# Gather, transform, scatter-add: later sort passes and smaller first one-hot groups

## The chip, the cores and the metric

The kernel runs on one core of one Trainium2 chip. The metric is the device time of one execution in microseconds (us). Times below are those of five runs (their median counts) and of one further, profiled execution, in which every instruction has a start and a duration.

## What is computed

A graph with 4096 nodes of 256 features and 262,144 edges: each edge carries its source node's features through a matrix, and the results are summed at its destination.

```python
def reference(nodes, edges_src, edges_dst, w_msg, w_self):
    N, D = nodes.shape
    self_out = nodes @ w_self
    src_feat = nodes[edges_src]
    msg = src_feat @ w_msg
    agg = np.zeros((N, D), dtype=np.float32)
    np.add.at(agg, edges_dst, msg)
    return (self_out + agg).astype(np.float32)
```

Node and weight values are normal random numbers, the edges' ends uniform random integers.

## The kernel before

**Idea.** The messages are first made per node, not per edge: Y = nodes · w_msg, in bf16. What is left is a sum over edges of rows of Y, which is a product of a matrix of edge counts with Y. The count matrix is cut into 352 *runs* (NRUN): 11 segments of 374 destinations (SW) by 32 blocks (NB) of 128 sources. Edges are sorted by run and destination. They lie in 2048 *chunks* of 128 edges, so that a chunk touches a narrow window of one or two runs. For each chunk the vector engine (DVE) makes two one-hot matrices, e (edge by source within its block, 128 wide) and d (edge by destination offset, 110 wide), and the tensor engine (PE) multiplies them into a window of the run's counts in PSUM.

**Stage 1, sort (to about 160 us of the span).** Edge keys stand as a 128 x 2048 fp32 array, and min/max passes on the DVE (`mm`, L746 and L749) with rotations by the PE bring them close to order. The last passes, SORT_S, work on two halves: chunks 0 to 1023 (XS) and 1024 to 2047 (XL). `_Sort.run` issues those of the first half at once. Those of the second half are 16 passes of one min and one max, 32 instructions; they are not issued but kept in the list `sort.late`.

**Stage 2, chunks.** One Python loop over c = 0 to 2047 writes out the order of all engines by hand (`manual_schedule`: each engine's instructions run in the order of the program). In it:

- `onehots(c, n)` makes the one-hots of a *group* of n chunks. `sizes` lists the groups: 8, 8, 16, three of 32, then 64s. A group of 32 or more takes per one-hot one subtraction (L396, `e_off` or `d_off`) and 8 (e) or 7 (d) comparisons (L402). e and d have three buffers each, one group to a buffer whatever its size, so the DVE can be at most three groups ahead. At some chunks (`split_at`), `split_vals` (L372, L373) first splits sorted keys `vals` into the two columns that the comparisons read.
- Sort passes of the second half: from group c = LATE_FROM on, four instructions of `sort.late` (LATE_STEP) stand behind each group's one-hots. At group LATE_SUB the list is empty, and `late.bases` (k16, the lowest key of each chunk, and gi) and `late.subtract` (L300) follow.
- `turn_late(0)`, at the clear of run SHIFT, and `turn_late(1)`, at chunk LATE_TURN, transpose the second half's keys by four PE instructions each into a free bank of the PSUM ring; ACT reads them into `vals` (L312). `late.total` is one more ACT pass over them (L343), for a test at the end. From run SHIFT on the ring of six banks is turned by one bank, so that one bank is free for the transposes.
- `late.places`, ten small DVE instructions, computes from gi the PSUM addresses (`poff`) of chunks 1024 and on. It stands ahead of group LATE_USE.
- For each chunk a matmul adds e^T d into the ring (L425). Runs are cleared ahead (a matmul by zeros, also L425), and evicted by ACT to bf16 buffers atr (L481) when the last chunk that can touch them is done; POOL issues a DMA that adds the overlap of a run into the next one (L501); 46 chunks later (LAG) the PE multiplies the run by Y into the output (L524, L519), to which nodes · w_self is added at the start of a segment (L513). Finished segments go out in 12 stores each on the SP queue, paced by later evictions.

**Behind the loop** stands a test whether the approximate sort was good enough, and a general path if not. Its instructions are placed among those of the loop by the framework's scheduler: k16 is written to DRAM (kd, L625) and read back shifted by one chunk (kn, L629) by DMAs on the SP queue, and the DVE's gn and v (L633, L635) read kn. In the kernel before, L633 and L635 stand directly behind the first e_off after the second half's `subtract`, and the second half's kd follows 27 output stores on the SP queue. In the changed kernel they stand behind the first e_off after `subtract` as well, and kd follows 36 output stores.

Of the kernel before, what the change touches and what calls it, by code (L numbers as in the profile page):

```python
# [24 lines left out]
NB = 32  # L25
JB = 16
HALF = 1024
SHIFT = 148
LATE_FROM = 256
LATE_STEP = 4  # L30
LATE_SUB = 768
LATE_TURN = 872
LATE_USE = 960
NSEG = 11
NRUN = NSEG * NB
OFF = 6 * (NB - 1)
# [47 lines left out]
def kernel(  # L84
# [14 lines left out]
    NCOL = E // P  # L99
# [81 lines left out]
    for (c0, c1), (d64, s64) in zip(PIECES, ld):  # L181
        dlo = d64[:].bitcast(I32)[:, 0::2]
        slo = s64[:].bitcast(I32)[:, 0::2]
        c = slice(c0, c1)
# [69 lines left out]
    sort = _Sort(nc, tc, psum_sort, XA, (XS, XL), id2, zw)  # L254
# [16 lines left out]
    class Half:  # L271
# [47 lines left out]
        def places(self):  # L319
# [6 lines left out]
            if self.h == 0:  # L326
                stt(
                    out=sl[:, c], in0=rhoc[:, c], scalar=float(SHIFT - OFF), in1=sl[:, c],
                    op0=ALU.is_ge, op1=ALU.add,
# [44 lines left out]

    split_at = {0: 64, 64: 512, 512: HALF, HALF: HALF + 256, HALF + 256: NCOL}

    sizes = [8, 8, 16, 32, 32, 32] + [64] * ((NCOL - 128) // 64)
    assert sum(sizes) == NCOL

    def onehots(c, n):  # L380
        res = []
        if c in split_at:
            split_vals(c, split_at[c])
        for nm, val, wid, row in (("e", slo_b, P, jrow), ("d", rel_b, W, drow)):
            o = ohp.tile([P, 32, wid, 2], BF16, name=nm + "_oh", tag=nm, bufs=3)
            v = val[:, c:c + n].rearrange("p (g i) -> p g i", i=2).unsqueeze(2)
            if n < 32:
                shp = [P, n // 2, wid, 2]
                tt(
                    out=o[:, 0:n // 2], in0=v.to_broadcast(shp),  # L390
                    in1=row[:].unsqueeze(1).to_broadcast(shp), op=ALU.is_equal,
                )
            else:
                u = ohp.tile([P, 32, JB, 2], I16, name=nm + "_off", tag="off", bufs=2)
                shp = [P, n // 2, JB, 2]
                tt(  # L396
                    out=u[:, 0:n // 2], in0=v.to_broadcast(shp),
                    in1=row[:, 0:JB, :].unsqueeze(1).to_broadcast(shp), op=ALU.subtract,
                )
                for j in range(0, wid, JB):  # L400
                    w = min(JB, wid - j)
                    tss(  # L402
                        out=o[:, 0:n // 2, j:j + w, :], in_=u[:, 0:n // 2, 0:w, :],
                        scalar=float(-j), op=ALU.is_equal,
                    )
            res.append(o)
        return res
# [5 lines left out]
    def clear_at(r):  # L413
        return min(max(line(at, r) for at in CLEAR[0:3]), line(CLEAR[3], r))

    def evac_at(r):
        return min(line(at, r + 1) for at in EVAC)
# [6 lines left out]
    def count_mm(ap, lhsT, rhs, start, after=()):  # L424
        mm = nc.tensor.matmul(  # L425
            out=ap, lhsT=lhsT, rhs=rhs, start=start, stop=True, skip_group_check=True,
        ).ins
        tc.declare_no_dep(
            mm, group="evac", keep=after, reason="disjoint banks by static schedule"
        )  # L430
        for i in after:
            tc.add_manual_dep(mm, i.name, DEP, reason="bank free")
        tc.add_to_no_dep_group("count", mm)
        last_mm[0] = mm
        return mm

    def bank(r):
        return (r + (r >= SHIFT)) % RING * BW

    def bank_free(slot):  # L440

        old = slot - RING
        if old == SHIFT:
            return [late_read[-1]]
        return [evac_of[old - (old > SHIFT)]] if old >= 0 else []

    late_read = []

    def turn_late(t):
        b = bank(SHIFT - 1) // BW  # L450
        b = (b + 1) % RING * BW
        mms, act = late.turn(t, ring[:, b:b + BW])
        for m in mms:
            after = bank_free(SHIFT) if t == 0 else [late_read[-1]]
            tc.declare_no_dep(
                m.ins, group="evac", keep=after, reason="disjoint banks by static schedule"
            )
            for i in after:
                tc.add_manual_dep(m.ins, i.name, DEP, reason="bank free")
            tc.add_to_no_dep_group("count", m.ins)  # L460
        ins = act.ins
        tc.declare_no_dep(
            ins, group="count", keep=[m.ins for m in mms], reason="disjoint banks by static schedule"
        )
        tc.add_manual_dep(ins, mms[-1].ins.name, DEP, reason="transposed")
        tc.add_to_no_dep_group("evac", ins)
        late_read.append(ins)

    def clear(r):
        b = bank(r)  # L470
        after = bank_free(r + (r >= SHIFT))
        zone = bass.AP(
            tensor=ring.tensor, offset=ring[:, b:b + 1].offset,
            ap=[list(ring[:].ap[0]), [SW + W - GAP, 2], [1, GAP]],
        )
        count_mm(zone, zer[:, 0, :], zer[:, 1:3, 0:GAP], True, after)

    def evac(r):
        at = ats[r % NAT]
        b = bank(r)  # L480
        ins = nc.scalar.copy(out=at[:, 0:SW + W], in_=ring[:, b:b + SW + W]).ins  # L481
        tc.declare_no_dep(
            ins, group="count", keep=[last_mm[0]], reason="disjoint banks by static schedule"
        )
        tc.add_manual_dep(ins, last_mm[0].name, DEP, reason="run complete")
        tc.add_to_no_dep_group("evac", ins)
        evac_of[r] = ins
        at_of[r] = at
# [4 lines left out]
    def by_dma(r):  # L493
        return r < NRUN - 8 and r // 2 % 6 > 0
# [54 lines left out]
    if True:  # L549
        todo = []  # L550
        regs = []
        ncl = 0
        nev = 0
        rest = sort.late
        starts = {}
        c = 0
        for n in sizes:
            starts[c] = n
            c += n
        for c in range(NCOL):  # L560
            if c in starts:
                c0 = c
                if c == LATE_USE:
                    late.places()
                e, d = onehots(c, starts[c])
                if c >= LATE_FROM:
                    for _ in range(LATE_STEP):
                        if rest:
                            rest.pop(0)()
                if c == LATE_SUB:  # L570
                    assert not rest
                    late.bases()
                    for t in range(2):
                        late.subtract(t)
            if c == LATE_TURN:
                turn_late(1)
                late.total()
            ci = c - c0
            while ncl < NRUN and clear_at(ncl) <= c:
                if ncl == SHIFT:  # L580
                    turn_late(0)
                clear(ncl)
                ncl += 1
            if c % 8 == 0:
                regs = [nc.tensor.alloc_register(f"po{c}_{i}") for i in range(8)]
                q, h8 = c % HALF // G8, c // HALF * G8
                nc.tensor.load(regs, poff[q:q + 1, h8:h8 + 8])
            addr = nc.tensor.snap(
                regs[c % 8], donate=True, min_val=PSUM0, max_val=PSUM0 + 4 * (RING * BW - W)
            ).with_bounds(  # L590
                min_val=PSUM0, max_val=PSUM0 + 4 * (RING * BW - W),
                guaranteed_mod_val=0, out_of_modulus=4,
            )
            off = (addr - PSUM0) // 4
            count_mm(
                ring[:, bass.ds(off, W)], e[:, ci // 2, :, ci % 2], d[:, ci // 2, :, ci % 2], False
            )
            for _ in range(FILL.get(c + 1, 0)):
                nc.tensor.matmul(  # L599
                    out=out_ps[:, 2:4, :], lhsT=zw[:, 0:P], rhs=zw[:], start=True, stop=True,  # L600
                    skip_group_check=True,
                )
            while nev < NRUN and (evac_at(nev) <= c or c == NCOL - 1):
                evac(nev)
                if nev % 2 == 0 and nev and by_dma(nev - 1):
                    merge(nev - 2)
                todo.append((c + LAG + (SWITCH if nev % NB == 0 else 0), nev))
                if nev % 2 and stores:
                    dst, src = stores.pop(0)
                    tc.add_manual_dep(  # L610
                        nc.sync.dma_start(dst, src).ins, evac_of[nev].name, DEP, reason="pace"
                    )
                nev += 1
            while todo and (todo[0][0] <= c or c == NCOL - 1):
                apply_run(todo.pop(0)[1])
# [382 lines left out]
```

## Time and profile before

| | |
|---|---|
| five runs | median 484.42 us, 481.81 to 488.24 |
| profiled execution | 483.58 us, span 481.8 us |
| mean TensorE clock in it | 0.959 |
| DVE busy | 416.2 us, 884 instructions |
| PE busy | 379.6 us, 4098 instructions |
| ACT busy | 240.5 us, 459 instructions |
| POOL busy | 195.2 us, 190 instructions |

The span runs from the first instruction to the last. A view called slices cuts it in 40 equal parts and gives each engine's busy share in tenths. The waits say for whom an engine stood idle and how long. The timeline lists instructions by start time, in us of the span: start, duration, engine, line, operation, what is written and read with the shapes, count, and in brackets the idle time before it and what ended it. Busy shares are averages over stages with different limits, so each stage must be read for itself.

### The profile page before, as it was taken

The page shows a single profiled execution, that of the slowest core. Times are in us where ns is not written, and L with a number is a line of the kernel's source. Part 1 is how long each engine was busy: PE and PEld are TensorE (multiplying, and loading weights), DVE is VectorE, ACT ScalarE, POOL GpSimd, SP SyncE. Part 2 cuts the span into 40 slices and gives each one's busy share as a digit, 9 for nine tenths or more (in the row PEclk, how much of TensorE's full clock was granted, in tenths as well). Part 3 has the DMA queues.
Part 4 walks back from the last instruction along what each step waited for, and adds up shares of the span by engine and source line. Part 5 has one row for each costly group of instructions (what it writes and reads, how often), then busy time and mean ns, then how long its engine had stood idle before and what let it go on. Part 6 is the DMA issues. An engine that isn't in the chain of part 4 may idle for free.

```text
span 481.8 us, 10985 instructions
## 1 busy us (share of the span) xinstructions
PE 379.6 (79%) x4098; PEld 310.4 (64%) x4107; DVE 416.2 (86%) x884; ACT 240.5 (50%) x459; POOL 195.2 (41%) x190
## 2 busy tenths in 40 slices
PE   0009736989871798987987987899999999999994
PEld 0004232745540468986876976789988899998893
DVE  8999999899899999999999997999978688897400
ACT  3100010322281236765654765577777677777771
POOL 4200000000000035764564675276667675776760
PEclk9999896999996799999998999899999999999999
DMA  8893111111000023443333334244544453545451
GB/s 324 119 180 110 27 26 25 28 23 27 12 0 0 0 16 26 31 48 38 31 41 35 36 30 58 26 45 44 53 42 52 40 57 36 56 40 56 38 60 40
DMA packets 66306, 23.78 MB, mean 49 GB/s; under 512 B 52170, under 2 KB 64970, under 8 KB 66250
## 3 DMA queue, kind: packets, MB, share of 16 engines
q0 software_dynamic: 43872, 10.42, 26.7%
q1 hardware_dynamic: 21548, 10.42, 8.2%
q10 hardware_dynamic: 830, 2.20, 1.2%
q8 instruction: 34, 0.56, 0.5%
q14 instruction: 22, 0.18, 0.1%
HBM read 8.92 MB, written 6.30 MB: 32 GB/s over the span
## 4 chain that ended last, share of the span: by engine, by line
DVE 44%; PE 40%; DMA 6%; issue 4%; POOL 2%; ACT 2%; SPq 0%; DVEq 0%; ACTq 0%; POOLq 0%
PE ring L425 15%; PE out_ps L524 13%; DVE XA L749 13%; DVE e_oh L402 8%; DVE d_oh L402 7%; PE warm L786 6%; DVE XS L749 6%; DVE XL L746 4%; DMA atr<-atr 3%; POOL atr L501 2%; PE tp_sw L892 2%; DMA d<-in_edges_dst_dram 2%; DVE d_off L396 2%; DVE e_off L396 1%; PE out_ps L599 1%
## 5 line engine op out<-in xcount | busy, mean ns | idle before, releaser
L501 POOL DMA_DIRECT2D atr<-atr x163 | 186.4, 1259 | 264.2 <-ACT atr L481 261.1
L481 ACT CAST atr<-ring 128x484 bf16<-128x484 f32 x352 | 192.3, 565 | 105.0 <-PE ring L425 84.1
L425 PE MATMUL ring<-d_oh,e_oh 128*128 128x110 bf16 x2048 | 196.3, 215 | 19.9 <-DVE d_oh L402 16.7
L425 PEld LDWEIGHTS <-e_oh 128*128 128x128 bf16 x2048 | 164.4, 98 | 25.6 <-issue 15.5
L524 PE MATMUL out_ps<-Y,atr 128*128 128x256 bf16 x1056 | 172.5, 275 | 2.2 <-DMA atr<-atr 2.2
L402 DVE TENSOR_SCALAR e_oh<-e_off 128x1024 bf16<-128x1024 int16 (+1 forms) x264 | 98.9, 445 | 20.5 <-PE ring L425 18.5
L786 PE MATMUL warm<-zw 128*128 128x512 bf16 x169 | 55.1, 421 | 65.6 <-DVE XA L749 49.9
L749 DVE TENSOR_TENSOR XA<-XA 128x510 f32<-128x510 f32 (+35 forms) x142 | 97.1, 731 | 5.0 <-ACT XA L896 3.3
L524 PEld LDWEIGHTS <-atr 128*128 128x128 bf16 x1056 | 90.7, 98 | 9.5 <-DMA atr<-atr 3.0
L425 PE MATMUL ring<-zer 128*128 128x204 bf16 x352 | 88.5, 252 | 1.4 <-ACT atr L481 1.3
L402 DVE TENSOR_SCALAR d_oh<-d_off 128x1024 bf16<-128x1024 int16 (+3 forms) x231 | 87.0, 446 | 1.1
L786 PEld LDWEIGHTS <-zw 128*128 128x128 bf16 x176 | 17.3, 102 | 99.6 <-issue 54.8
L896 ACT COPY XA<-tp_sw 128x512 f32<-128x512 f32 x24 | 14.2, 593 | 92.1 <-PE tp_sw L892 91.4
L425 PEld LDWEIGHTS <-zer 128*128 128x128 bf16 x352 | 34.4, 98 | 9.5 <-issue 6.9
L749 DVE TENSOR_TENSOR XS<-XS 128x512 f32<-128x512 f32 (+17 forms) x40 | 29.0, 770 | 2.6 <-ACT XS L950 2.0
L746 DVE TENSOR_TENSOR XL<-XL 128x1196 f32<-128x1196 f32 (+15 forms) x32 | 28.1, 918 | 0.3
L892 PEld LDWEIGHTS tp_sw<-XA,id 128*128 128x128 f32 x192 | 22.4, 190 | 5.2 <-issue 2.4
L892 PE MATMUL tp_sw<-XA,id 128*128 128x128 f32 x192 | 23.9, 277 | 2.1 <-DVE XA L749 2.1
L396 DVE TENSOR_TENSOR e_off<-slo_b,jrow 128x1024 int16<-128x1024 int16 (+1 forms) x33 | 21.6, 655 | 0.0
L396 DVE TENSOR_TENSOR d_off<-rel_b,drow 128x1024 int16<-128x1024 int16 (+1 forms) x33 | 21.5, 652 | 0.0
L643 DVE COPY bsum<-ring 1x3 f32<-1x3 f32 x1 | 0.1, 149 | 24.1 <-PE ring L642 24.1
L519 PE MATMUL out_ps<-Y,atr 128*128 128x256 bf16 x65 | 17.8, 274 | 0.0
(104 smaller groups left out, 153.4 us busy)
## 6 DMA issues: line engine op xcount, KB each, us to landing
atr<-atr POOLq DMA_DIRECT2D x123, 55.0 KB, 2.8
out_dram<-o_sb SPq DMA_DIRECT2D x110, 32.0 KB, 1.6
nodes_bf<-in_nodes_dram POOLq DMA_DIRECT2D x1, 2048.0 KB, 15.8
nodes_bf_dram<-nodes_bf SPq DMA_DIRECT2D x1, 2048.0 KB
atr<-atr POOLq DMA_DIRECT2D x40, 27.5 KB, 2.9
s<-in_edges_src_dram ACTq DMA_DIRECT2D x2, 512.0 KB
d<-in_edges_dst_dram SPq DMA_DIRECT2D x2, 512.0 KB, 8.1
XT<-nodes_bf_dram SPq DMA_TRANSPOSE x64, 2.4
```

The lines of the kernel that those rows point to most:

```text
L396: tt(out=u[:, 0:n // 2], in0=v.to_broadcast(shp), in1=row[:, 0:JB, :].unsqueeze(1).to_broadcast(shp), op=ALU.subtract,)
L402: tss(out=o[:, 0:n // 2, j:j + w, :], in_=u[:, 0:n // 2, 0:w, :], scalar=float(-j), op=ALU.is_equal,)
L425: mm = nc.tensor.matmul(out=ap, lhsT=lhsT, rhs=rhs, start=start, stop=True, skip_group_check=True,).ins
L481: ins = nc.scalar.copy(out=at[:, 0:SW + W], in_=ring[:, b:b + SW + W]).ins
L501: nc.gpsimd.dma_start(out=atr[:, b:b + n, 0:W], in_=atr[:, a:a + n, SW:SW + W], accum_op=ALU.add)
L519: nc.tensor.matmul(out=out_ps[:, 0, :], lhsT=spill[:, SW:SW + P], rhs=Y[:, b, :], start=False, stop=False, skip_group_check=True,)
L524: nc.tensor.matmul(out=out_ps[:, t, :], lhsT=at[:, t * P:(t + 1) * P], rhs=Y[:, b, :], start=False, stop=(b == NB - 1), skip_group_check=True,
L746: self.defer.append(lambda: self.nc.vector.tensor_tensor(out=out, in0=in0, in1=in1, op=op))
L749: self.nc.vector.tensor_tensor(out=out, in0=in0, in1=in1, op=op),
L786: self.nc.tensor.matmul(out=w[:], lhsT=self.zw[:, 0:P], rhs=self.zw[:], start=True, stop=True).ins
L892: self.nc.tensor.matmul(out=tp[:, g * P:(g + 1) * P], lhsT=self.turned(rots[8 * h + 4 * t + g]), rhs=sel(x)[:, 4 * t + g], start=True, sto ...
L896: self.nc.scalar.copy(out=sel(y)[:, 4 * t:4 * t + 4], in_=tp[:].rearrange("p (g i b) -> p g i b", g=4, b=bb),)
```

## The change

The sort passes of the second half stand behind later groups. They are no longer four to a group from 256 on: after group c of n chunks, (c + n - 352) / 544 of the 32 instructions are due. With the new group sizes these are 5, 4, 4, 3, 4, 4, 4 and 4, behind groups 384, 448, 512, 576, 640, 704, 768 and 832; before, they were four each behind the groups 256 to 704. bases and subtract stand behind group 896 instead of 768. The run at whose clear the ring is turned and the first four transposes stand is 165 instead of 148, which puts them at chunk 957 instead of 857; the other four are at 970 instead of 872. places stands ahead of group 1024 instead of 960. Chunks 128 to 319 and 1024 to 1151 are made in groups of 32 instead of 64, which are ten groups for five. Nothing else changes.

```diff
-SHIFT = 148
-LATE_FROM = 256
-LATE_STEP = 4
-LATE_SUB = 768
-LATE_TURN = 872
-LATE_USE = 960
+SHIFT = 165
+LATE_FROM = 352
+LATE_SUB = 896
+LATE_TURN = 970
...
-    sizes = [8, 8, 16, 32, 32, 32] + [64] * ((NCOL - 128) // 64)
+    sizes = [8, 8, 16] + [32] * 9 + [64] * 11 + [32] * 4 + [64] * 14
...
-        rest = sort.late
+        ops, done = sort.late, 0
...
-                if c == LATE_USE:
+                if c == HALF:
                     late.places()
                 e, d = onehots(c, starts[c])
                 if c >= LATE_FROM:
-                    for _ in range(LATE_STEP):
-                        if rest:
-                            rest.pop(0)()
+                    due = len(ops) * (c + starts[c] - LATE_FROM) // (LATE_SUB - LATE_FROM)
+                    for op in ops[done:due]:
+                        op()
+                    done = max(done, min(due, len(ops)))
                 if c == LATE_SUB:
-                    assert not rest
+                    assert done == len(ops)
                     late.bases()
```

## The prediction

> **What bounds the kernel now.** I read the span in slices first. The vector engine (DVE) is full from the start to about slice 26, and only then is the tensor engine (PE) full.
>
> ```profile
> PE   0009736989871798987987987899999999999994
> DVE  8999999899899999999999997999978688897400
> ```
> (A slice is 12.05 us. Slices 13 to 26, 160 to 320 us, are the ones that the change touches.) The waits of 160 to 482 us tell who starves whom; columns are total us, times, longest:
>
> ```profile
> DVE e_oh L402 <- PE ring L425: 18.5, 13, 3.2
> PE ring L425 <- DVE d_oh L402: 16.7, 10, 3.1
> DVE gn L633 <- DMA kn<-kd: 2.7, 1, 2.7
> ```
> Ten times the PE waits for one-hots, 13 times the DVE waits for the PE to free a buffer. The timelines separate them: all PE waits lie between 166 and 302 us, all DVE ones after 339 us. This is the last wait of the PE:
>
> ```profile
> 301.56 0.26 PE L425 MATMUL ring<-d_oh,e_oh 128*128 128x110 bf16 x2 [2.77 <-DVE d_oh L402]
> ```
> Counting ring matmuls, it is the start of chunk 832. So up to chunk 832 the DVE's queue sets the pace, from there the PE does (180 us to the end). At chunk 960 the DVE's one-hots were ready 5.7 us before the PE came, at 1024 7.2 us. The question is only whether the DVE's sum of work ahead of *any* group shrinks, and which group is the last that the PE waits for.
>
> The DVE's timeline prices its pieces (start, duration, then the group):
>
> ```profile
> 178.19 0.41 DVE L396 TENSOR_TENSOR e_off<-slo_b,jrow 128x512 int16<-128x512 int16 x1
> 178.71 1.71 DVE L402 TENSOR_SCALAR e_oh<-e_off 128x512 bf16<-128x512 int16 x8
> 182.19 0.68 DVE L396 TENSOR_TENSOR e_off<-slo_b,jrow 128x1024 int16<-128x1024 int16 x1
> 189.37 0.68 DVE L396 TENSOR_TENSOR e_off<-slo_b,jrow 128x1024 int16<-128x1024 int16 x1
> 203.51 5.22 DVE L746 TENSOR_TENSOR XL<-XL 128x1196 f32<-128x1196 f32 x4
> 208.64 0.69 DVE L396 TENSOR_TENSOR e_off<-slo_b,jrow 128x1024 int16<-128x1024 int16 x1
> 290.57 1.29 DVE L300 SCALAR_TENSOR_TENSOR XL<-XL,gi 128x512 f32<-128x512 f32 x2
> 295.18 0.18 DVE L633 TENSOR_SCALAR gn<-kn 128x16 int32<-128x16 int32 x1 [2.71 <-DMA kn<-kd]
> ```
> A group of 32 chunks takes 4.00 us from its e_off to the next (178.19 to 182.19); a group of 64 takes 7.18 (182.19 to 189.37), 7.1 as the mean of 14 such groups. The eight quartets of sort passes take 5.13, 4.53, 3.64, 3.27, 3.04, 2.84, 2.67, 2.57 us: 27.7 in all.
>
> [...] from start to start, a 1024-element L402 takes 338 ns in the median, a 512-element one 202, so half the elements cost 60%. [...] of the three 32-chunk groups two took 4.00 us, and the one under which POOL issued three DMAs 5.07. [...] Here the clock fell after waits of 3.15, 2.81 and 2.77 us, not after 2.33: windows of 10 us at 220 and 230 us show 0.85 and 0.98, which is 3.4 us at half speed, 1.7 us lost.
>
> **The change part by part.** (1) *Six new 32-chunk groups for three 64-chunk ones* (chunks 128 to 320), and *four for two* at 1024 to 1152. POOL's disturbance is per chunk: 64-chunk groups average 0.6 over their undisturbed 6.5, so I take 4.0 + 0.3 = 4.3 per 32 (bounds 4.0 and 5.07, the two measured). The early part then costs the DVE 6 x 4.3 - 3 x 7.1 = +4.5 us (+2.7 to +9.1), on the path. What is gained is that the PE may start on half a group: its 1.62 us wait at chunk 128 goes.
>
> (2) *Sort passes.* The formula puts 5, 4, 4, 3, 4, 4, 4, 4 of them behind groups 384 to 832; before it was four each behind 256 to 704. They are moved by two groups, hardly spread. No DVE work is saved; what is ready ahead of them is ready earlier, what follows is not.
>
> (3) *bases and subtract* (289.34 to 291.78, 2.45 us) go from group 768 to 896. With them goes the wait at L633: the gn of the closing test still stands behind the next e_off and waits for kd and kn, two DMAs in series that begin when k16 is done (290.36; landed 295.1). It stays 2.7 us (0 to 5). In SP's queue they now follow 36 stores instead of 27; the 36th is paced by run 127's eviction, near chunk 756, long past. The stores behind them have no reader on chip.
>
> (4) *places* (ten small instructions, 1.56 us with those of the test between them) goes behind group 960, where the DVE will wait for vals anyway: -1.56 ahead of 960.
>
> (5) *Transposes.* Two times four on the PE (0.45 us each) at chunks 957 and 970 instead of 857 and 872, and three ACT instructions (0.69, 0.69, 1.15 + 0.19) with them. 17 evictions of 0.565 us move ahead of them on ACT. Before, the eviction after total came late and the PE waited 1.30 us for its bank at 311.94; I move this cost, too. New is a DVE wait: split_vals of chunk 1024 now needs the ACT read that follows PE chunk 970. Queued behind it are all later one-hots; who waits is the PE at 1024.
>
> The recurrence, in us of the span: DVE ready = previous ready + passes behind it + 7.1 (+0.45 for a split_vals); PE start = the later of that and previous start + 8.5 (the PE's 64 chunks, waits taken out, over 320 to 1024), +1.7 after a wait over 2.7. Chunk 128's group starts on the DVE at 182.2, so 320's at 182.2 + 25.8 = 208.0.
>
> | chunk | passes before it | DVE ready | PE arrives | PE starts | before |
> |---|---|---|---|---|---|
> | 320 | 0 | 215.1 | 213.4 | 215.1 | 215.9 |
> | 384 | 0 | 222.2 | 223.6 | 223.6 | 227.3 |
> | 448 | 6.3 | 235.6 | 232.1 | 235.6 | 238.3 |
> | 512 | 4.3 | 247.5 | 245.8 | 247.5 | 248.8 |
> | 576 | 3.55 | 258.1 | 256.0 | 258.1 | 259.9 |
> | 640 | 2.45 | 267.7 | 266.6 | 267.7 | 270.5 |
> | 704 | 3.05 | 277.8 | 276.2 | 277.8 | 279.8 |
> | 768 | 2.85 | 287.8 | 286.3 | 287.8 | 289.5 |
> | 832 | 2.7 | 297.6 | 296.3 | 297.6 | 301.6 |
> | 896 | 2.55 | 307.2 | 306.1 | 307.2 | 314.0 |
> | 960 | 2.45 + 2.7 + 0.3 | 319.8 | 316.2 | 319.8 | 323.0 |
>
> The 6.8 us ahead at 896 are half lost at 960: with the passes, bases and the kn wait so late, the PE waits 3.6 us there, and its clock falls. 1024: the PE arrives at 319.8 + 8.5 + 0.45 + 1.3 + 1.7 = 331.7 (before 331.9). Its chunk 970 is reached some 2.1 us after 319.8; transposes 0.9 at half clock, ACT 1.0, split_vals 0.45, 4.3: one-hots ready at 328.5, so the new wait (bound: 0 to 2 us of PE time, as ACT may be two evictions late) costs nothing; PE work of 960 covers it. Then 332.8, 337.1, 341.4 and, for the 64-chunk group 1152, 348.5; the PE needs 8.0 + 8.4 us for 128 chunks and arrives at 348.1. It starts at 348.5, before 348.3. From there both kernels do the same with the DVE ahead.
>
> **Sum:** +0.2 us on a span of 481.8; the profiled run took 483.58 (1.8 outside the span) and the median of five is 484.42, 0.8 above it. Forecast: 484.42 + 0.2 = **484.6**.
>
> **Rivals.**
> - *Much slower: the 32-chunk groups cost as the disturbed one, 5.07.* One mechanism, at ten groups: POOL's DMAs hold up twice as many instructions. For: the only group measured beneath three POOL issues. Against: two of three at 4.00, and issues come per run, not per instruction. Each 0.1 us costs up to 1.0; from 4.8 us per group it decides (+5 us, 489.6); at 5.07, 492.3. Chance 0.14.
> - *Faster: the DVE's lead holds to 960.* If kn lands before gn asks for it and 32-chunk groups run at 4.0, 960 is ready at 319.8 - 2.7 - 1.8 = 315.3, where the PE arrives at 314.4 and keeps its clock; with 8.5 + 0.45 + 1.3 and 16.45 it reaches 1152 at 342.0: 484.4 - 6.3 = 478.1. For: small groups start under few POOL issues. Against: kd and kn took 4.8 us and nothing shortens them. Halfway, 481.3. Chance 0.10 for over 1%.
> - *It does not do what it says*: passes only shifted, early groups hidden, waits merely renamed: 484.4, inside the forecast's range. Chance 0.10.
>
> **Numbers.** The forecast has 0.66 (its own range 482 to 487.5). One per cent, 4.8 us, is about what a measurement of this kernel tells from no change, as its five runs span 6.4. Faster 0.10, within 0.75, slower 0.15 (rival one and a tail of the forecast). Range 480.5 to 489.5: it leaves out the ends of both rivals.
>
> **What would show it.** PE starts near 298 at 832 and 307 at 896 show step 2; a last long PE wait at 960, about 3.6 us, with half clock behind it, shows step 3; DVE 4.3 us per 32-chunk group shows step 1; no PE wait at 1024 and at most 1 us at 1152 show step 5. It is wrong if groups 128 to 320 take the DVE over 29 us, if gn does not wait, or if the PE stands at 1024 for vals.

## The result and the profile after

The changed kernel takes 486.49 us in the median of 41 runs (483.94 to 488.40), the kernel before 484.02 in 78 runs beside it. The ratio is 1.0056, 95% interval 1.0041 to 1.0070: 2.7 us slower (2.0 to 3.4). A second comparison of the same two kernels, later, gave 1.0061 (1.0041 to 1.0081). The profiled execution shows none of this in its length: its span is 481.8 us, as before the change. Single executions scatter by more than the difference, as experiments 7 and 8 will show, so what follows compares stages, and the sizes of effects are taken from the timed runs.

The slices of the span after the change, PE and DVE:

```profile
PE   0009736989871799979968969879999999999994
DVE  8999999899899999999999999879999998887400
```

In slices 26 and 27, counted from 1 (301 to 325 us), the DVE, full there before, has holes, and behind them it stays full to slice 33 (398 us), where before it began to have time to spare at slice 30 (349 us). The waits of 160 to 482 us (us in total, times, longest) say what the holes are:

```profile
PE ring L423 <- DVE d_oh L400: 19.9, 12, 4.1
DVE e_oh L400 <- PE ring L423: 7.0, 5, 1.8
DVE gn L632 <- DMA kn<-kd: 2.6, 1, 2.6
DVE slo_b L370 <- ACT vals L310: 2.2, 1, 2.2
```

The PE waits for one-hots 3.2 us longer in all than before, and the DVE for the PE 11.5 us less: the time in which the DVE sets the pace has become longer. The wait for kn is still there; a wait of this length for the late keys (`vals`) is new. The last waits of the PE, in its timeline (start, duration, group, idle before it):

```profile
298.61 0.26 PE L423 MATMUL ring<-d_oh,e_oh 128*128 128x110 bf16 x2 [0.24 <-DVE d_oh L400]
308.17 0.26 PE L423 MATMUL ring<-d_oh,e_oh 128*128 128x110 bf16 x2 [1.32 <-DVE d_oh L400]
320.26 0.44 PE L423 MATMUL ring<-d_oh,e_oh 128*128 128x110 bf16 x3 [3.43 <-DVE d_oh L400]
349.41 0.21 PE L423 MATMUL ring<-d_oh,e_oh 128*128 128x110 bf16 x1 [0.80 <-DVE d_oh L400]
```

Counted off among the ring matmuls these are chunks 832, 896, 960 and 1152. Before, the last such wait was at 832, at 301.56. Beside the forecast's table:

| chunk | PE forecast | PE measured | before |
|---|---|---|---|
| 384 | 223.6 | 225.5 | 227.3 |
| 448 | 235.6 | 235.7 | 238.3 |
| 832 | 297.6 | 298.6 | 301.6 |
| 896 | 307.2 | 308.2 | 314.0 |
| 960 | 319.8 | 320.3 | 323.0 |
| 1024 | 331.7 | 332.0 | 331.9 |
| 1152 | 348.5 | 349.4 | 348.3 |

The PE is 5.8 us ahead of the kernel before at chunk 896 and 1.1 behind it at 1152. The DVE's timeline shows the two places where that is lost. First a small group, and the start of the first 64-chunk group behind six of them:

```profile
182.09 0.42 DVE L394 TENSOR_TENSOR e_off<-slo_b,jrow 128x512 int16<-128x512 int16 x1
182.62 1.98 DVE L400 TENSOR_SCALAR e_oh<-e_off 128x512 bf16<-128x512 int16 x8
184.51 0.41 DVE L394 TENSOR_TENSOR d_off<-rel_b,drow 128x512 int16<-128x512 int16 x1
184.96 1.49 DVE L400 TENSOR_SCALAR d_oh<-d_off 128x512 bf16<-128x512 int16 x7
186.36 0.42 DVE L394 TENSOR_TENSOR e_off<-slo_b,jrow 128x512 int16<-128x512 int16 x1
...
208.44 0.67 DVE L394 TENSOR_TENSOR e_off<-slo_b,jrow 128x1024 int16<-128x1024 int16 x1
```

Six groups take 208.44 - 182.09 = 26.35 us, 4.39 each (4.28 to 4.48). The same 192 chunks took 21.3 before (from 182.19 to 203.51): +5.0 us. Then the end of the second half's preparation:

```profile
310.49 0.68 DVE L394 TENSOR_TENSOR e_off<-slo_b,jrow 128x1024 int16<-128x1024 int16 x1
313.77 0.17 DVE L632 TENSOR_SCALAR gn<-kn 128x16 int32<-128x16 int32 x1 [2.60 <-DMA kn<-kd]
...
323.95 0.23 DVE L370 TENSOR_SCALAR slo_b<-vals 128x256 int16<-128x256 int16 x1 [2.17 <-ACT vals L310]
324.22 0.42 DVE L394 TENSOR_TENSOR e_off<-slo_b,jrow 128x512 int16<-128x512 int16 x1
```

gn stands inside group 960's one-hots, so the PE, which waits for them, waits for two DMAs. The PE does not wait for `vals` at chunk 1024: its one-hots are complete at 328.66, and the PE comes at 332.00. But from 323.95 on the DVE has no hole up to chunk 1152, where the PE waits 0.80 us for it, so part of that wait may go back to `vals`. No run takes this wait away alone.

### The profile page after: what moved, and what is told of

Read it like the earlier page. It is cut to its first block, busy times and chain, and to the rows that moved or that the text cites. A ratio compares the mean times of both kernels' runs of the same rounds, so it can differ in the third digit from the quotient of the medians.

```text
span 481.8 us, 11076 instructions
## 1 busy us (share of the span) xinstructions
PE 379.8 (79%) x4098; PEld 311.2 (65%) x4107; DVE 423.7 (88%) x969; ACT 240.5 (50%) x459; POOL 195.2 (41%) x190
## 4 chain that ended last, share of the span: by engine, by line
DVE 56%; PE 33%; DMA 4%; issue 3%; ACT 2%; POOL 1%; SPq 0%; DVEq 0%; ACTq 0%; POOLq 0%
DVE XA L748 14%; DVE e_oh L400 13%; PE ring L423 12%; DVE d_oh L400 11%; PE out_ps L522 11%; DVE XS L748 6%; DVE XL L745 6%; PE warm L785 5%; PE tp_sw L891 2%; DVE d_off L394 2%; DVE e_off L394 2%; DMA d<-in_edges_dst_dram 2%; PE out_ps L598 1%; DMA atr<-atr 1%; ACT XA L895 1%
## 5 line engine op out<-in xcount | busy, mean ns | idle before, releaser
L400 DVE TENSOR_SCALAR e_oh<-e_off 128x1024 bf16<-128x1024 int16 (+1 forms) x304 | 103.3, 410 | 10.4 <-PE ring L423 7.0
L400 DVE TENSOR_SCALAR d_oh<-d_off 128x1024 bf16<-128x1024 int16 (+3 forms) x266 | 89.6, 407 | 1.3
```

What stands on the lines that cost most here:

```text
L400: tss(out=o[:, 0:n // 2, j:j + w, :], in_=u[:, 0:n // 2, 0:w, :], scalar=float(-j), op=ALU.is_equal,)
```

## The experiments

Ratios are to the kernel before, run beside it on the same chip. Where a diff says "sizes", it is the list of group sizes.

**1. The shift without the small groups.** The changed kernel, with

```diff
-    sizes = [8, 8, 16] + [32] * 9 + [64] * 11 + [32] * 4 + [64] * 14
+    sizes = [8, 8, 16, 32, 32, 32] + [64] * ((NCOL - 128) // 64)
```

> The changed kernel with the group sizes of the kernel before (8, 8, 16, three of 32, then 64s); the later sort passes, bases, transposes and places stay. Theory 'small groups cost, the shift gains': in the changed kernel's trace the DVE begins group 320 at 208.4 us, before (without its sort passes) at 203.5, so 4.9 us of DVE work go; group 960 is ready near 315.3, the PE waits about 3 us there, and reaches chunk 1152 near 344 against 348.3 before: about 4.4 us under the kernel before, ratio 0.991. Rival 'the shift is what costs' (the late wait at 960, the split of the late keys): no better than the changed kernel, ratio 1.005 or more.

Measured: 0.9954 (0.9928 to 0.9981), 2.2 us *faster* than the kernel before. The rival falls: the later passes do not cost, they gain. Seen from the changed kernel, taking its ten small groups back is worth 4.9 us (1.0056 to 0.9954). In the trace the PE still waits at 960, for 2.45 us, and goes from its first ring matmul to chunk 1152 in 177.3 us (182.05 before, 183.2 after). The timed gain is half of what was expected.

**2. Small groups alone**, in the kernel before:

```diff
-    sizes = [8, 8, 16, 32, 32, 32] + [64] * ((NCOL - 128) // 64)
+    sizes = [8, 8, 16] + [32] * 9 + [64] * 27
```

> The kernel before with chunks 128 to 319 in six groups of 32 and nothing else changed. Theory 'small groups cost': the DVE sets the pace up to chunk 832, so its 4.9 us more arrive there whole; the PE starts chunk 832 near 306.5 instead of 301.6: ratio 1.010. Rival 'an earlier start of the PE pays for them': the PE is ahead from chunk 128 on and the ratio is 1.000.

Measured: 1.0095 (1.0057 to 1.0132), +4.6 us, as the first theory said. This run was not clean, which I saw later: four passes stand behind each *group* from 256 on, so the small groups 256 and 288 took four each and pulled the rest up by one group.

**3. and 4. gn away from the path.** In the changed kernel (3) and the one before (4), the test's first instruction waits for an eviction late in the loop, so the scheduler places it far down; nothing is left out:

```diff
-    tss(out=gn[:], in_=kn[:], scalar=7, op=ALU.arith_shift_right)
+    gn_late = tss(out=gn[:], in_=kn[:], scalar=7, op=ALU.arith_shift_right).ins
+    tc.add_manual_dep(gn_late, evac_of[300].name, DEP, reason="test late")
```

> The changed kernel with the closing test's gn (and v behind it) made to wait for a late eviction (run 300), so that it stands far down in the DVE's order and no longer between e_off and e_oh of group 960. Theory 'the wait for kn is on the path': 2.6 us of wait and 0.3 of instructions go ahead of 960, which is ready near 317.3 when the PE arrives at 317.1; no half clock behind it; the PE then waits about 2 us at chunk 1152 and starts it near 345 instead of 349.4: some 4 us under the changed kernel, ratio 0.996 to the kernel before. Rival 'covered': the PE or the late keys bound it there anyway, ratio 1.005 as for the changed kernel.

> The kernel before with the same edit on gn and nothing else. Theory: the last wait of the PE, 2.77 us at chunk 832, is the wait for kn and no more; without it group 832 is ready at 298.6, the PE arrives at 298.8 and keeps its full clock: 2.8 + 1.7 us less, ratio 0.990. Rival 'another wait takes its place' (the eviction that waited 1.3 us at 311.9, the merge DMA at 320): ratio 0.996 or more.

Measured: 1.0021 (1.0003 to 1.0039) for the changed kernel, 1.7 us under its 1.0056; 0.9947 (0.9930 to 0.9964) for the one before, 2.5 us faster. Both directions are as expected, the sizes some half. The PE's timeline of the kernel before with gn late:

```profile
298.69 0.26 PE L425 MATMUL ring<-d_oh,e_oh 128*128 128x110 bf16 x2 [0.24 <-DVE d_oh L402]
307.21 0.26 PE L425 MATMUL ring<-zer 128*128 128x204 bf16 x1 [1.30 <-ACT atr L481]
```

Chunk 832 now waits 0.24 us instead of 2.77; the 1.30 us wait for an eviction, which was at 311.94, has stayed. So the wait for kn made up nearly all of the last wait of the kernel before, and the change kept it.

**5. The four late small groups taken back**, in the changed kernel:

```diff
-    sizes = [8, 8, 16] + [32] * 9 + [64] * 11 + [32] * 4 + [64] * 14
+    sizes = [8, 8, 16] + [32] * 9 + [64] * 27
```

> The changed kernel with chunks 1024 to 1151 in two groups of 64 again; the six early groups of 32 stay. Theory 'the four late small groups bring nothing': vals are split at 323.95 us, a 64-chunk group is ready near 331.4, where the PE comes at 332.0, the next ones at 338.6 and 345.8, ahead of the PE, and the 0.8 us wait at chunk 1152 goes: 0.8 us under the changed kernel, ratio 1.004. Rival 'they are needed for the start at 1024': the PE waits there, ratio 1.007 or more.

Measured: 1.0057 (1.0034 to 1.0080). The trace has no PE wait for one-hots at 1024 or 1152, but the time can't be told from the changed kernel's. The 0.8 us expected lie below what this comparison resolves. That these groups are not needed for the start at 1024 is shown by the trace.

**6. Shift and late gn together**, with the old sizes (edits of 1 and 3).

> The later sort passes with the old group sizes and gn behind a late eviction, two edits that gained 2.2 and 2.5 us each alone. Theory: in the run with the old sizes the PE still waited 2.1 us at chunk 960 and lost 1.7 at half clock; without the kn wait both go, 1024 waits 0.6 for the late keys, 3.2 us less: ratio 0.989. Rival 'both took away the same wait': ratio 0.995.

Measured: 0.9901 (0.9869 to 0.9934), the fastest of all, 1% under the kernel before. Its PE timeline at chunks 896 and 960:

```profile
304.55 0.26 PE L423 MATMUL ring<-d_oh,e_oh 128*128 128x110 bf16 x2 [1.29 <-DVE d_oh L400]
314.23 0.32 PE L423 MATMUL ring<-d_oh,e_oh 128*128 128x110 bf16 x3 [0.83 <-DVE d_oh L400]
```

The wait at 960 falls from 3.43 (changed) over 2.45 (shift only) to 0.83 us. The two gains add (2.2 and 2.5 us alone, 4.8 together); they were not the same wait.

**7. and 8. Both kernels once more**, unchanged, for second profiled executions.

> The kernel before unchanged, for a second profiled execution beside the others of this call. If single executions scatter by chance: from the first ring matmul to chunk 1152 again near 182.0 us, from there to the end of the span between 132 and 135. Ratio 1.000.

> The changed kernel unchanged, for a second profiled execution. Theory 'the first one was lucky in its last part': first ring matmul to chunk 1152 again near 183.2 us, from there to the end 133.5 to 134.5 instead of 132.4, ratio 1.006. Rival 'the time is lost ahead of 1152 and the first profile missed it': 185 us or more to chunk 1152.

Measured: 0.9997 (0.9968 to 1.0026) and 1.0061. From the first ring matmul to chunk 1152, and from there to the end of the span:

| | to 1152 | from 1152 |
|---|---|---|
| before, first and second profile | 182.05, 178.55 | 133.46, 133.44 |
| after, first and second profile | 183.22, 183.70 | 132.37, 135.56 |

The changed kernel repeats itself up to 1152. Behind it 133.5 to 134.5 was expected, and its two profiles lie on either side: 132.4 was lucky, 135.6 unlucky (the second one has 2.0 us of PE waits for merge DMAs, the first 0.2). The kernel before did *not* repeat itself, which I had not expected. In its first profile chunk 768 to 896 took 24.5 us, in the second 22.0. A window of 10 us around the start of chunk 832, in the first profile of the kernel before (columns: window, length, busy us of PE, PE weight load, DVE, ACT and POOL with counts, PE clock, DMA share, GB/s):

```profile
300.00:310.00 10.00, 8.24 (x85) 7.29 (x85) 9.75 (x33) 4.49 (x8) 3.96 (x4) 0.83 0.36 34
```

The same window in its second profile:

```profile
300.00:310.00 10.00, 7.23 (x91) 6.63 (x90) 9.76 (x36) 6.20 (x11) 4.65 (x5) 1.00 0.38 37
```

The first execution lost clock behind its wait of 2.77 us (a mean clock of 0.83 over 10 us is 3.4 us at half speed), the second, behind 2.11 us, did not (1.00). Of the 3.5 us between the two at chunk 1152, 1.9 lie between chunks 832 and 896, where this happened; 0.8 lie ahead of 832 and 0.7 in the 64 chunks from 896, where only the first waited for merge DMAs. The kernel of experiment 10 is the kernel before up to chunk 1408 and so gives a third execution: it waited 2.77 us at 832 and took 180.5 us to chunk 1152. The mean of the three is 180.4.

**9. Twice the small groups**, in the kernel before.

```diff
+    sizes = [8, 8, 16] + [32] * 15 + [64] * 24
```

> The kernel before with chunks 128 to 511 in twelve groups of 32: twice the dose of the run with six. Theory 'each pair of small groups costs the DVE 1.6 us and the PE all of it': six more groups, twice 4.6 us, ratio 1.019. Rival 'the PE's earlier start pays from some point on': ratio 1.012 or less.

Measured: 1.0292 (1.0247 to 1.0337), neither value. The cause was my edit: with four passes behind each small group, all 32 stood ahead of chunk 512, where they delay the PE by 19 us; at chunk 1152 some 12 us of it are left (192.6 us from the first ring matmul, against 180.4). Experiments 11 and 12 leave the passes where they were.

**10. The same small groups where the PE sets the pace**, chunks 1408 to 1599 of the kernel before.

```diff
+    sizes = [8, 8, 16, 32, 32, 32] + [64] * 20 + [32] * 6 + [64] * 7
```

> The kernel before with chunks 1408 to 1599 in six groups of 32, where the PE sets the pace and the DVE waits for buffers. Theory 'only the place makes them dear': the DVE has some 1.4 us to spare per 64 chunks and is three groups ahead, so nothing is lost: ratio 1.000, at most 1.002. Rival 'small groups cost the PE or POOL themselves': ratio 1.005 to 1.010.

Measured: 0.9994 (0.9968 to 1.0021). Its waits of 345 to 482 us show the cover, 14.5 us in which the DVE still waits for the PE:

```profile
DVE e_oh L402 <- PE ring L425: 14.5, 4, 6.0
```

**11. and 12. Six and twelve small groups with the passes kept behind every 64 chunks**, in the kernel before.

```diff
-                if c >= LATE_FROM:
+                if c >= LATE_FROM and (c + starts[c]) % 64 == 0:
```

> As the run with six early groups of 32 in the kernel before, but the four sort passes stand behind every 64 chunks, where they stood before, and not behind every group; in the earlier run the two small groups at 256 and 288 had taken four each, which pulled all later passes up by one group. Theory 'the price lies in the groups themselves': 4.9 us more DVE work ahead of chunk 832 as in the earlier run, ratio 1.009. Rival 'the pulled-up passes were the cost': 1.003 or less.

> The same with twelve small groups (chunks 128 to 511) and the passes kept in their places. Theory: without the pulled-up passes the dose is linear, 9.8 us of DVE work, ratio 1.019 to 1.020. Rival 'more than linear by itself' (smaller lead, three groups of 32 are 96 chunks): 1.025 or more, as in the earlier run with twelve.

Measured: 1.0097 (1.0058 to 1.0135) and 1.0184 (1.0148 to 1.0220), +4.7 and +8.9 us: linear within their intervals (1.8 us either way), some 0.75 us for each small group. Set beside experiment 9, this shows that what went beyond it there came from the pulled-up passes.

Together, of about 482.4 us: shift -2.2, six early small groups +4.6, four late ones nothing that can be told; the sum +2.4 stands against 2.7 measured, well within the intervals.

## Why the prediction was right in its steps and low in its number

The forecast was 484.6, +0.2 us, with a range of 480.5 to 489.5 and 0.75 on "within 1%". The time was +2.7 us, 486.5. By its steps:

1. *Six small groups, +4.5 us, on the path.* Right: +5.0 in the trace (4.39 per group, not 4.3), +4.7 in the clean run alone. That the PE's earlier start gives nothing back was right, too: its wait at chunk 128 went, and the one at 320 grew from 1.02 to 2.83 us. The rival with 5.07 per group is wrong. POOL issued two or three DMAs beneath each of the six, and none took more than 4.48; so three issues alone do not make 5.07, and what did stays open.
2. *Passes moved, no work saved.* Right to 1.2 us in the first profile at every chunk of the forecast's table but 384, which came 1.9 us late: the longer wait at 320 was followed by half clock (0.50 from 216.65 to 220.06 us), which the forecast did not have there. The DVE set the start of 448 all the same. The prediction didn't say what experiment 1 shows: the shift alone is a gain of 2.2 us, and the small groups are what turned it.
3. *gn still waits 2.7 us.* Right, 2.60, and the last long wait of the PE, forecast 3.6 at 960, is 3.43. Experiments 3, 4 and 6 show that it is on the path in both kernels. The rival in which kn is early did not come about.
4. *places costs nothing at 1024.* Right: it ends at 321.8, and the DVE then waits for `vals` until 323.95.
5. *Late transposes, no PE wait at 1024; at most 1 us at 1152.* Right in the first profile: none, and 0.80 (1.13 in the second). That the row of 1024 came out within 0.3 us was partly luck. The forecast added 1.3 us for the eviction and 1.7 for half clock, but the two cover each other. Where the clock was kept at 960, in experiment 3 (0.26 us for a pair of ring matmuls, 0.39 at half clock in the changed kernel) and experiment 5 (granted clock 1.00 from 316 to 327 us), the PE does wait for that eviction, 1.15 and 1.14 us, and needs 11.0 us for the 64 chunks. This is experiment 3:

```profile
323.05 0.26 PE L423 MATMUL ring<-zer 128*128 128x204 bf16 x1 [1.15 <-ACT atr L479]
```

In the changed kernel's two profiles the half-speed PE comes later, the wait is gone, and it needs 11.7 us with 6.8 us at half speed and 11.4 with 3.4. Half clock cost 0.4 us for 3.4 there and 0.7 for 6.8, not 1.7 and 3.4.

The term that made the forecast low is in the sum, not in a mechanism: "It starts at 348.5, before 348.3". The 348.3 came from one execution, in which the last wait was followed by half clock (0.50 from 302.14 to 305.55 us). I took that as a property of the kernel before. Experiments 7 and 10 show that it is not: from the first ring matmul to chunk 1152 its instructions took 182.1, 178.6 and 180.5 us, 180.4 in the mean. The changed kernel took 183.2 and 183.7, where 182.3 was forecast (348.5 less the 166.2 at which the first ring matmul starts). The means differ by 3.1 us, near the measured 2.7. So of the forecast's error at chunk 1152 some 1.7 us lie in the time taken for the kernel before, and 1.2 in the changed kernel's own: small groups 0.5 us dearer, the wait at 1152 longer by 0.4 and 0.7. With so few executions this split is an estimate. Half clock at 960 is no fixed property of the changed kernel either: the run of experiment 5, the same up to chunk 1023, kept its clock there (1.00).

Experiments 1 and 4 gained only half of what was expected for the same reason, in part. Their own times to chunk 1152 were foreseen, 177.8 and 177.6 us, and came out at 177.3 and 177.0; what was too long was the 182.1 with which they were compared. Against 180.4 they gain 3.1 and 3.4 us there; behind 1152 they take 1.0 and 0.7 us more than the kernel before (134.4 and 134.2 against 133.5), and why is open. For experiment 3 the reason doesn't hold, as it was expected against the changed kernel. Its trace reaches 1152 2.7 us earlier than that kernel's first profile, where 4.4 was expected; in it the DVE still waits 1.49 us for `vals` and the PE 1.13 at 1152. Why only 1.7 us of this arrive in the timed runs is open.

## What to carry to other kernels

Where one engine's queue set the pace here, splitting its instructions so that a consumer may start earlier was paid in full, and linearly up to twelve groups (+4.7 us for six, +8.9 for twelve); the same split where the other engine set the pace was free (0.9994). Before moving work within such a queue, look for instructions in it that wait for something slow and that nobody needs yet, as gn for a DMA here: moving that one instruction (-2.5 us) gave as much as moving all the sort passes (-2.2 us). A recurrence worked out from a trace held to a microsecond or two, but the execution that it is compared with has its own luck: two profiles of one kernel lay 3.5 us apart at chunk 1152, more than the whole change is worth. And two costs at one place should not be added before it is seen that neither hides the other, as half clock hid the wait for the eviction here (1.15 us where the clock was kept).

## What the runs showed of the hardware

Whether the PE's clock falls behind a wait is not settled by the wait's length. The wait of 2.81 us at chunk 576 was followed by half clock in the first profile of the kernel before and in the run with gn late (a mean clock of 0.83 from 260 to 270 us in both), but not in the second profile of the kernel before (1.00). At 960, 3.43 and 3.42 us brought it in the two profiles of the changed kernel, 3.19 us in the run without late small groups did not. The prediction's rule, 1.7 us lost behind every wait over 2.7, fails on this.

It matters where the idle time of a wait falls. In the clock records of the first profiles of both kernels the stretches of half clock between 148 and 470 us begin whole multiples of 3.41 us apart: at 148.54, 227.05, 261.18 and 302.14 us before the change, at 148.38, 216.65, 247.37 and 319.05 us after it. Cut along this grid, with the columns as above, the wait at chunk 832 fell into one window in the first profile of the kernel before (idle time is the length less the PE's busy time, 2.77 us), and the next one ran at half clock:

```profile
298.73:302.14 3.41, 0.64 (x10) 0.57 (x9) 3.33 (x9) 0.49 (x2) 2.86 (x3) 1.00 0.41 45
302.14:305.55 3.41, 3.41 (x26) 2.79 (x25) 3.35 (x9) 1.12 (x2) 0.25 (x1) 0.50 0.17 23
```

In the run without late small groups the 3.19 us at chunk 960 fell across a border, with 1.94 us of idle time in the first window and 1.63 in the second, and the clock stayed:

```profile
316.47:319.88 3.41, 1.47 (x17) 1.24 (x16) 3.38 (x10) 1.27 (x3) 1.51 (x1) 1.00 0.62 101
319.88:323.30 3.42, 1.79 (x21) 1.47 (x21) 2.67 (x17) 1.12 (x2) 1.01 (x1) 1.00 0.00 1
323.30:326.71 3.41, 2.27 (x30) 1.98 (x29) 2.46 (x8) 3.15 (x6) 0.75 (x2) 1.00 0.26 26
```

In the second profile of the changed kernel the 3.42 us left 2.01 in one window:

```profile
319.37:322.78 3.41, 1.40 (x17) 1.09 (x17) 3.05 (x18) 1.12 (x2) 0.62 (x1) 1.00 0.14 16
322.78:326.19 3.41, 3.41 (x24) 2.73 (x23) 1.72 (x9) 2.43 (x5) 0.57 (x1) 0.50 0.24 21
```

In its first profile the 3.43 us left 2.22 in one window and 1.21 in the next, which ran at half clock already, and the window behind that did so, too:

```profile
315.64:319.05 3.41, 1.19 (x15) 0.98 (x13) 3.38 (x9) 1.19 (x2) 1.19 (x1) 1.00 0.49 80
319.05:322.46 3.41, 2.20 (x17) 1.97 (x17) 2.63 (x17) 1.05 (x2) 1.01 (x1) 0.50 0.00 0
322.46:325.88 3.42, 3.42 (x24) 2.75 (x23) 1.83 (x9) 2.60 (x6) 0.18 (x1) 0.50 0.24 21
```

A count over the first profiles of both kernels, 88 such windows in each from 166 to 470 us, agrees, with idle time as the profile counts it. Of the windows at full clock, the six in which the PE was idle for 2.15 us or more were followed by one at half clock, and the 163 with 1.62 us or less were not. Of those at half clock, the one with 1.21 us idle was followed by another at half clock, and the six with 0.54 or less were not. With the windows shown from the other runs, 1.94 us is the most idle time that left the clock, and 2.01 the least that half clock followed. So by these figures a wait between 2.0 and some 3.9 us (twice 1.94, an estimate) may bring half clock or not, according to where the grid lies in that execution. This is the luck that the comparison of single profiles had in it.
